# Storing the first tile of a contrast kernel in eight strided pieces with growing packets

## Chip, cores, metric

The kernel runs on one core of a Trainium2 chip. The metric is the device time in microseconds, as a median of runs. The profiled span, from the first instruction to the last, is about 2 us shorter (237.3 us in the run of the kernel before that took 239.14). In the trace, q1 is the queue of loads (issued by SP, the SyncE engine) and q10 the queue of stores (issued by ACT). Both run on the same 16 DMA engines: in the kernel before, their packets sum to 98.9% of 16 engines' span, and about 16 are in flight from 3 to 234 us. A packet is one record of a DMA engine's work in the trace; here it moves one contiguous piece of one row (for tile 0's 128 rows, stored in two column parts, 128 packets of 8 KB and 128 of 24 KB). Packet records lie in the trace file, and no view of the profile prints them one by one; numbers said to be from them were read there.

## The reference

```python
# x: 16 x 3 x 512 x 512 float32, factor = 1.5
mean = np.mean(x, axis=(2, 3), keepdims=True)
return np.clip(mean + factor * (x - mean), 0, 1).astype(np.float32)
```

There are 48 images of 1 MiB. All bytes must come in once and go out once, 100.66 MB in total. An image can be clipped only when all of it has been summed.

## The kernel before

Four images make a tile of 128 rows of 8192 floats (4.19 MB, 32 KB a row), so there are 12 tiles. They pass through a ring of six tile buffers. DVE (VectorE) sums a part of each row, ACT (ScalarE) the rest, PE (TensorE) turns the row sums into one shift per row, and DVE multiplies, adds and clips in place. Tile 0 is clipped and stored in two column parts, 2048 and 6144 wide.

```python
SHORT = 2048
FIRST = (SHORT, ROW - SHORT)
SUM = 4352
# ... (cut)
    def compute(t):
        xt = ring[:, t % BUFS, :]
        own = sums[:, 2 * t : 2 * t + 2]
        nc.vector.tensor_reduce(out=own[:, 0:1], in_=xt[:, 0:SUM], axis=mybir.AxisListType.X, op=Alu.add)
        nc.scalar.activation(out=junk, in_=xt[:, SUM:ROW], func=Act.Copy, accum_out=own[:, 1:2])
        # ... two matmuls into shift (cut)
        c = 0
        for n in FIRST if t == 0 else [ROW]:
            # ... mult-add, then clip, of columns c to c + n (cut)
            store(t, c, c + n)          # nc.scalar.dma_start: ACT issues it
            c += n
# ... (cut)
        load(0, c1=SHORT)               # nc.sync.dma_start: SP issues it
        load(0, c0=SHORT)
        load(1)
        load(2, n=2)                    # two tiles in one DMA
        load(4, n=2)
        for t in range(n_tiles):
            compute(t)
            if t + BUFS < n_tiles:
                load(t + BUFS)          # waits until tile t has left the buffer
```

Of the kernel before, what the change touches and what calls it, by code (L numbers as in the profile page):

```python
# [1 line left out]

# [4 lines left out]


P = 128  # L10
ROW = 8192
BUFS = 6
SHORT = 2048
FIRST = (SHORT, ROW - SHORT)
SUM = 4352


@with_exitstack
def kernel(
    ctx: ExitStack,  # L20
    tc: tile.TileContext,
    x: bass.AP,
    factor: float,
    out: bass.AP,
):



    nc = tc.nc
    f32 = mybir.dt.float32  # L30
    Alu = mybir.AluOpType
    Act = mybir.ActivationFunctionType

    B, C, H, W = x.shape
    n_img, n_pix = B * C, H * W
    ppi = n_pix // ROW
    per_tile = P // ppi
    n_tiles = n_img // per_tile
    assert ppi * ROW == n_pix and per_tile * n_tiles == n_img

    factor = float(factor)
    wconst = (1.0 - factor) / float(n_pix)

    x_f = x.rearrange("b c h w -> (b c h w)")
    out_f = out.rearrange("b c h w -> (b c h w)")

    def dram(ap, t, c0=0, c1=ROW):
        return bass.AP(tensor=ap.tensor, offset=t * P * ROW + c0, ap=[[ROW, P], [1, c1 - c0]])

    consts = ctx.enter_context(tc.tile_pool(name="consts", bufs=1))  # L50
    xpool = ctx.enter_context(tc.tile_pool(name="xpool", bufs=1))
    small = ctx.enter_context(tc.tile_pool(name="small", bufs=1))
    psum = ctx.enter_context(tc.tile_pool(name="psum", bufs=1, space=bass.MemoryType.PSUM))


    sums = small.tile([P, 2 * n_tiles], f32, name="sums")
    junk = small.tile([P, ROW - SUM], f32, name="junk")
    bias = psum.tile([P, n_tiles], f32, name="bias")

    blockw = consts.tile([P, P], f32, name="blockw")  # L60
    nc.gpsimd.memset(blockw, 0.0)  # L61
    for a in range(0, P, ppi):
        nc.gpsimd.memset(blockw[a : a + ppi, a : a + ppi], wconst)  # L63


    ring = xpool.tile([P, BUFS, ROW], f32, name="ring")

    def load(t, c0=0, c1=ROW, n=1):

        b = t % BUFS  # L70
        src = bass.AP(
            tensor=x_f.tensor,
            offset=t * P * ROW + c0,
            ap=[[ROW, P], [P * ROW, n], [1, c1 - c0]],
        )
        nc.sync.dma_start(out=ring[:, b : b + n, c0:c1], in_=src)  # L76
# [4 lines that stand above are left out]
        nc.vector.tensor_reduce(  # L81
            out=own[:, 0:1], in_=xt[:, 0:SUM], axis=mybir.AxisListType.X, op=Alu.add
        )
        nc.scalar.activation(out=junk, in_=xt[:, SUM:ROW], func=Act.Copy, accum_out=own[:, 1:2])  # L84
        shift = bias[:, t : t + 1]
        nc.tensor.matmul(shift, blockw, own[:, 1:2], start=True, stop=False)  # L86
        nc.tensor.matmul(shift, blockw, own[:, 0:1], start=False, stop=True)  # L87
        c = 0
        for n in FIRST if t == 0 else [ROW]:
            part = xt[:, c : c + n]  # L90
            nc.vector.tensor_scalar(  # L91
                out=part, in0=part, scalar1=factor, scalar2=shift, op0=Alu.mult, op1=Alu.add
            )
            nc.vector.tensor_scalar(  # L94
                out=part, in0=part, scalar1=0.0, scalar2=1.0, op0=Alu.max, op1=Alu.min
            )
            store(t, c, c + n)
            c += n

    def store(t, c0, c1):  # L100
        nc.scalar.dma_start(out=dram(out_f, t, c0, c1), in_=ring[:, t % BUFS, c0:c1])

    with tc.manual_schedule():
        load(0, c1=SHORT)
        load(0, c0=SHORT)
        load(1)
        load(2, n=2)
        load(4, n=2)
        for t in range(n_tiles):
            compute(t)  # L110
            if t + BUFS < n_tiles:
                load(t + BUFS)


# [1 line left out]
_INS = ['x', 'factor']  # L116
_OUTS = [((16, 3, 512, 512), 'float32')]

_NUMBERS = {'factor': 1.5}


# [26 lines left out]
```

## Time and profile before

| | kernel before |
|---|---|
| time, median of 3 runs | 239.27 us (239.07 to 239.33) |
| profiled span | 237.3 us |
| DVE busy, idle waiting for loads | 163.1 us, 45.7 us |
| first store issued | 20.91 us |
| ACT starts its sum of tile 1 | 28.08 us |
| last load landed, last clip done | 203.73 us, 218.1 us |

DVE waits for loads in its sums (busy time, mean ns of one | idle time before them):

```profile
L81 DVE TENSOR_REDUCE sums<-ring 128x1 f32<-128x4352 f32 x12 | 56.2, 4683 | 45.7 <-DMA ring<-in_x_dram 45.7
```

These lines of the timeline (start, duration, engine, line, work) are where the change acts:

```profile
20.91 7.06 ACTq L101 DMA_DIRECT2D out_dram<-ring  x2
...
28.08 3.40 ACT L84 ACTIVATE junk<-ring 128x3840 f32<-128x3840 f32 x1 [11.70 <-DVE ring L94]
...
41.94 0.34 ACTq L101 DMA_DIRECT2D out_dram<-ring  x1
```

ACT issues the two stores of tile 0 between 20.91 and 27.97 us, sums its part of tile 1 at once, and issues the store of tile 1 at 41.94 us.

### The profile page before, as it was taken

What the parts mean: (1) busy time and instruction counts of PE and PEld (TensorE: products, weight loads), DVE (VectorE), ACT (ScalarE), POOL (GpSimd) and SP (SyncE); (2) the same over time, 40 slices, a digit from 0 to 9 for tenths busy, and PEclk for the clock granted to TensorE, in tenths of its full rate; (3) what the DMA queues carried; (4) which work ended last, traced back from release to release, by engine and by line L of the source; (5) the groups of instructions that cost most, each with busy time, mean ns of one, the idle gap of its engine ahead of it and who ended that gap; (6) DMA issues with size and microseconds to landing.
All of it is one profiled execution on the core that took longest, in us unless ns stands there. A gap on an engine that the chain in (4) does not pass through costs nothing.

```text
span 237.3 us, 285 instructions
## 1 busy us (share of the span) xinstructions
PE 14.1 (6%) x48; PEld 12.0 (5%) x48; DVE 163.1 (69%) x38; ACT 43.2 (18%) x25; POOL 0.9 (0%) x9
## 2 busy tenths in 40 slices
PE   0010010001010001010010100100100100010000
PEld 0010010001010001010010100100100100010000
DVE  0079989048989328999989898891892795687000
ACT  2050230041050023050320504101400500500000
POOL 1000000000000000000000000000000000000000
DMA  7999999999999999999999999999999999999996
GB/s 297 410 442 442 421 442 359 456 439 441 442 436 414 403 431 442 442 442 442 436 442 436 414 409 425 442 442 442 442 436 442 436 420 403 425 442 442 442 442 265
DMA packets 3712, 100.66 MB, mean 424 GB/s; under 512 B 384, under 2 KB 384, under 8 KB 384
## 3 DMA queue, kind: packets, MB, share of 16 engines
q1 hardware_dynamic: 1840, 50.33, 49.7%
q10 hardware_dynamic: 1872, 50.33, 49.2%
HBM read 50.33 MB, written 50.33 MB: 424 GB/s over the span
## 4 chain that ended last, share of the span: by engine, by line
DMA 57%; DVE 29%; another core or an unknown queue 3%; PE 1%; SPq 1%; issue 0%; DVEq 0%
DMA ring<-in_x_dram 41%; DMA out_dram<-ring 16%; DVE sums L81 10%; DVE ring L91 9%; DVE ring L94 9%; PE bias L87 1%; SPq L76 1%; DVEq L91 0%
## 5 line engine op out<-in xcount | busy, mean ns | idle before, releaser
L81 DVE TENSOR_REDUCE sums<-ring 128x1 f32<-128x4352 f32 x12 | 56.2, 4683 | 45.7 <-DMA ring<-in_x_dram 45.7
L84 ACT ACTIVATE junk<-ring 128x3840 f32<-128x3840 f32 x12 | 40.8, 3403 | 163.3 <-DMA ring<-in_x_dram 107.5
L91 DVE TENSOR_SCALAR ring<-ring,bias 128x8192 f32<-128x8192 f32 (+2 forms) x13 | 54.1, 4163 | 8.9 <-PE bias L87 7.4
L94 DVE TENSOR_SCALAR ring<-ring 128x8192 f32<-128x8192 f32 (+2 forms) x13 | 53.3, 4099 | 0.4
L86 PE MATMUL bias<-sums,blockw 128*128 128x1 f32 x24 | 7.0, 361 | 190.8 <-ACT junk L84 190.8
L86 PEld LDWEIGHTS bias<-sums,blockw 128*128 128x128 f32 x24 | 6.0, 312 | 191.7 <-ACT junk L84 175.2
L87 PE MATMUL bias<-sums,blockw 128*128 128x1 f32 x24 | 7.0, 363 | 4.3 <-DVE sums L81 3.9
L87 PEld LDWEIGHTS bias<-sums,blockw 128*128 128x128 f32 x24 | 6.0, 311 | 5.3 <-DVE sums L81 5.0
L84 ACT ACTIVATION_READ_ACCUMULATOR junk<-ring 128x1 f32 x12 | 2.2, 186 | 0.0
L84 ACT ACT_TABLE_LOAD x1 | 1.3, 1283 | 0.7 <-PEq L129 0.7
L63 POOL MEMSET blockw<- 32x32 f32 x4 | 0.5, 117 | 0.2
L61 POOL MEMSET blockw<- 128x128 f32 x1 | 0.2, 204 | 0.3 <-POOLq L129 0.3
L129 POOL MEMSET const-bfloat16-1.0<- 128x1 bf16 x1 | 0.1, 111 | 0.0
L129 POOL MEMSET const-uint8-127<- 128x1 uint8 x1 | 0.1, 111 | 0.0
L129 POOL MEMSET const-float32-1.0<- 128x1 f32 x1 | 0.1, 108 | 0.0
L129 POOL MEMSET const-float32-0.0<- 128x1 f32 x1 | 0.1, 103 | 0.2 <-issue 0.2
## 6 DMA issues: line engine op xcount, KB each, us to landing
out_dram<-ring ACTq DMA_DIRECT2D x11, 4096.0 KB, 35.8
ring<-in_x_dram SPq DMA_DIRECT2D x7, 4096.0 KB, 49.7
ring<-in_x_dram SPq DMA_DIRECT2D x2, 8192.0 KB, 66.7
ring<-in_x_dram SPq DMA_DIRECT2D x1, 3072.0 KB, 11.7
out_dram<-ring ACTq DMA_DIRECT2D x1, 3072.0 KB, 28.2
ring<-in_x_dram SPq DMA_DIRECT2D x1, 1024.0 KB, 4.8
out_dram<-ring ACTq DMA_DIRECT2D x1, 1024.0 KB, 17.5
```

The lines of the kernel that those rows point to most:

```text
L61: nc.gpsimd.memset(blockw, 0.0)
L63: nc.gpsimd.memset(blockw[a : a + ppi, a : a + ppi], wconst)
L76: nc.sync.dma_start(out=ring[:, b : b + n, c0:c1], in_=src)
L81: nc.vector.tensor_reduce(out=own[:, 0:1], in_=xt[:, 0:SUM], axis=mybir.AxisListType.X, op=Alu.add)
L84: nc.scalar.activation(out=junk, in_=xt[:, SUM:ROW], func=Act.Copy, accum_out=own[:, 1:2])
L86: nc.tensor.matmul(shift, blockw, own[:, 1:2], start=True, stop=False)
L87: nc.tensor.matmul(shift, blockw, own[:, 0:1], start=False, stop=True)
L91: nc.vector.tensor_scalar(out=part, in0=part, scalar1=factor, scalar2=shift, op0=Alu.mult, op1=Alu.add)
L94: nc.vector.tensor_scalar(out=part, in0=part, scalar1=0.0, scalar2=1.0, op0=Alu.max, op1=Alu.min)
L129: nc = _bacc.Bacc("TRN2", target_bir_lowering=False, num_devices=1)
```

## The change

Its intent, as far as the code tells: the first stores meet loads that have the engines to themselves, and small packets should let them in gently. Tile 0 leaves in eight DMAs of 32 rows each (every 4th row), whose packets grow from 4 KB to 32 KB. All are issued after the whole clip. The two paired loads become four single ones.

```diff
-FIRST = (SHORT, ROW - SHORT)
+RAMP = [            # first row, row step, first column, last column
+    (0, 4, 0, 1024),
+    (1, 4, 0, 2048),
+    (0, 4, 1024, 4096),
+    (2, 4, 0, 4096),
+    (2, 4, 4096, ROW),
+    (0, 4, 4096, ROW),
+    (1, 4, 2048, ROW),
+    (3, 4, 0, ROW),
+]
 ... (cut: tile 0's mult-add and clip are no longer split)
+        for piece in RAMP if t == 0 else [(0, 1, 0, ROW)]:
+            store(t, *piece)
-    def store(t, c0, c1):
-        nc.scalar.dma_start(out=dram(out_f, t, c0, c1), in_=ring[:, t % BUFS, c0:c1])
+    def store(t, q=0, parts=1, c0=0, c1=ROW):
+        dst = bass.AP(tensor=out_f.tensor, offset=(t * P + q) * ROW + c0,
+                      ap=[[parts * ROW, P // parts], [1, c1 - c0]])
+        nc.scalar.dma_start(out=dst, in_=ring[q::parts, t % BUFS, c0:c1])
 ... (cut)
-        load(2, n=2)
-        load(4, n=2)
+        for t in range(2, BUFS):
+            load(t)
```

More of the change, by code (lines that the diff above doesn't have):

```diff
@@ L45 @@
     out_f = out.rearrange("b c h w -> (b c h w)")
-    def dram(ap, t, c0=0, c1=ROW):
-        return bass.AP(tensor=ap.tensor, offset=t * P * ROW + c0, ap=[[ROW, P], [1, c1 - c0]])
     consts = ctx.enter_context(tc.tile_pool(name="consts", bufs=1))
@@ L87, in compute @@
         nc.tensor.matmul(shift, blockw, own[:, 0:1], start=False, stop=True)
-        c = 0
-        for n in FIRST if t == 0 else [ROW]:
-            part = xt[:, c : c + n]
-            nc.vector.tensor_scalar(
-                out=part, in0=part, scalar1=factor, scalar2=shift, op0=Alu.mult, op1=Alu.add
-            )
-            nc.vector.tensor_scalar(
-                out=part, in0=part, scalar1=0.0, scalar2=1.0, op0=Alu.max, op1=Alu.min
-            )
-            store(t, c, c + n)
-            c += n
-    def store(t, c0, c1):
-        nc.scalar.dma_start(out=dram(out_f, t, c0, c1), in_=ring[:, t % BUFS, c0:c1])
+        nc.vector.tensor_scalar(
+            out=xt, in0=xt, scalar1=factor, scalar2=shift, op0=Alu.mult, op1=Alu.add
+        )
+        nc.vector.tensor_scalar(
+            out=xt, in0=xt, scalar1=0.0, scalar2=1.0, op0=Alu.max, op1=Alu.min
+        )
+        for piece in RAMP if t == 0 else [(0, 1, 0, ROW)]:
+            store(t, *piece)
+    def store(t, q=0, parts=1, c0=0, c1=ROW):
+        dst = bass.AP(
+            tensor=out_f.tensor,
+            offset=(t * P + q) * ROW + c0,
+            ap=[[parts * ROW, P // parts], [1, c1 - c0]],
+        )
+        nc.scalar.dma_start(out=dst, in_=ring[q::parts, t % BUFS, c0:c1])
     with tc.manual_schedule():
```

## The prediction

> **What bounds the kernel now.** I read the page first for busy shares, then the DMA view, then stretches of time, then the chain, and last the timeline of the first 75 us, where the change is.
>
> From the page, busy time of the engines and the DMA rows:
>
> ```profile
> PE 14.1 (6%) x48; PEld 12.0 (5%) x48; DVE 163.1 (69%) x38; ACT 43.2 (18%) x25; POOL 0.9 (0%) x9
> ...
> DMA  7999999999999999999999999999999999999996
> ...
> DMA packets 3712, 100.66 MB, mean 424 GB/s; under 512 B 384, under 2 KB 384, under 8 KB 384
> ...
> q1 hardware_dynamic: 1840, 50.33, 49.7%
> q10 hardware_dynamic: 1872, 50.33, 49.2%
> ```
>
> No compute engine is above 69%. The loads (q1) take 49.7% and the stores (q10) 49.2% of 16 DMA engines' span: 98.9% of 237.3 us, or 234.7 us. Only the first and the last slice are below 9. The trace's packet records say the same: the first load packet starts at 1.74 us, the last store packet ends at 236.05 us, and in each microsecond from 3 to 234 about 16 packets are in flight. So the transfers never pause.
>
> Is a packet's cost fixed? Three stretches (last columns: share of the 16 engines, GB/s):
>
> ```profile
> 56.00:60.00 4.00, 0.00 (x1) 0.00 (x0) 3.89 (x1) 0.00 (x0) 0.00 (x0) 1.00 0.91 393
> 80.00:84.00 4.00, 0.00 (x0) 0.00 (x0) 0.00 (x0) 0.00 (x0) 0.00 (x0) 1.00 0.91 393
> 172.00:176.00 4.00, 0.00 (x0) 0.00 (x0) 3.97 (x2) 0.00 (x0) 0.00 (x0) 1.00 0.91 393
> ```
>
> A packet is booked where it starts, so 0.91 is no idling: 393 GB/s over 4 us is 48 packets of 32 KB, and 0.91 x 64 engine-us / 48 is 1.21 us each, with DVE busy or idle. The packet records give median 309 ns for 8 KB, 912 ns for 24 KB and 1213 ns for 32 KB, loads and stores alike. A line through them is 7.7 ns + 36.8 ns per KB of 1,000 bytes.
>
> The chain of waits ends in the last tile:
>
> ```profile
> 154.17 49.57 DMA ring<-in_x_dram
> 203.73 0.02 issue
> 203.76 4.70 DVE sums L81
> ...
> 209.18 4.50 DVE ring L91
> 213.69 0.02 issue
> 213.71 4.43 DVE ring L94
> ```
>
> The last load lands at 203.73 us and the last clip ends at 218.1 us. That chain stops at the last compute instruction, but the transfers run on to 236 us. At 218.1 us the engines still owe 18 us x 0.43 MB/us (16 packets of 32,768 bytes in 1.213 us), about 7.7 MB: the last tile (4.19 MB) and most of the one before. So the last compute ends far earlier than it need, and the time is first packet plus packet time plus tail.
>
> [...] the 8 KB store packets of 24.6 to 36.9 us come about 1.52 us apart on an engine, which is 309 + 1213 ns, one store packet per load packet. Small store packets thus yield bandwidth to loads; they do not waste it. [...]
>
> **The change, part by part.**
>
> *Clip of tile 0.* Two mult-adds and two clips (1.29, 1.23, 3.42 and 3.36 us in the timeline) become one of each (4.49 and 4.43 us, from tile 1's rows). The sum falls from about 9.2 to 8.9 us, and tile 0 is clipped at 18.33 + 8.95 = 27.3 us, not 27.5. But the first store leaves at 27.3 instead of 20.91 us. Loads fill those 6.4 us, since one queue alone keeps the engines busy (12 to 21 us had loads only).
>
> *Packets of tile 0's stores.* Before: 128 of 8 KB and 128 of 24 KB, 256 packets. After: eight DMAs of 32 rows, again 256 packets with the same 4.19 MB. By the line above their engine time is identical: (256 x 7.7 ns + 4.19 MB x 36.8 ns per KB) / 16 is 9.8 us in both. The two 8 MB loads become four of 4 MB; their packets stay 32 KB. Added are 32 DMAs' completion writes instead of 24, one of 9 ns per engine each: 8 x 9 ns = 0.07 us.
>
> *Waits at issue.* In the built program the DMAs share eight completion semaphores in turn, and a DMA waits for the earlier user of its own. With six more stores these waits move into ACT's queue: the sixth piece waits for the load of tile 1, the seventh for the first piece to land, the eighth for the third. ACT works in order, so tile 1's reduction stands behind the eighth piece. I replayed one DMA engine by hand, alternating load and store packets with the durations above, and with 3.7 us from issue to a store's first packet (before: issue 20.91, first packet 24.64). It lands piece one at about 34, piece three at 40.5 and piece eight at 61 us. So ACT starts tile 1 near 41 us instead of 28.08, and tile 1's store is issued near 41 + 4.9 (ACT start to mult-add, 28.08 to 32.95) + 9 = 55 us instead of 41.94. That is 13 us lost on compute. But piece eight's packets last to about 60 us, and on the load side tiles 3, 4 and 5 (issued after the first load, tile 2 and piece two land, about 6, 32 and 37 us) last to 70 us. Neither queue dries.
>
> *Loads 6 on.* Load 6 waits for all of tile 0 to have left, about 61 us instead of 56. Load 5 then still has some 9 us of packets. In return tile 4 need no longer wait for a paired load: before, an 8.20 us wait ended at 87.56 us. Tile 4 should be loaded by about 60 us and DVE should lead again by tile 5.
>
> *Sum.* Nothing is saved in packet time, +0.07 us of completion writes, first packet and tail as they are: 239.27 + 0.1 = about 239.4 us.
>
> **The rivals.** (a) *The smaller first packets help*: loads get ahead, compute starts earlier, and time falls. For it: the DVE idles 45.7 us on loads. Against it: what is idle is not the bound; the most that a perfect order could win is 237.3 - 234.5 (all packets on 16 engines) = 2.8 us, 1.2%, and 1.74 us of it is before the first packet, which the change doesn't touch. It would make 238.5 us. (b) *ACT's new wait becomes the bound*: 13 us lost on tile 1 reach the end if both queues run dry. Against it: the queued loads last past 70 us, and the end has slack: tile 11 could be clipped 9 us later and still be stored in time. With this wholly on the path the time would be 250 us; I give it 2%. (c) *The 32-row stores run slower*: no trace here says which rows go to which engine. [...] Worst case every packet of tile 0's stores takes twice as long: +9.8 us. [...] I give any visible loss 12%. (d) *Unequal engines*: if the rows spread unevenly, some engines end late; two rows on each make this unlikely.
>
> **Range and chances.** Three runs of before lie within 0.26 us, and the packet sum admits no gain beyond 1.2%, so faster by over 2% is nearly excluded: 0.01. Slower by over 2% (over 244 us) needs (b) or a bad (c): 0.03. The rest, 0.96, is the same. The range reaches down 0.6 us for another order at the tail or another chip, and up 1 us for a mild (c): 238.8 to 240.4 us.
>
> **What would show it right or wrong.** Right: q1 plus q10 near 234.6 us of 16 engines; every DMA slice between the first and the last at 9; the first store issued near 27.4 us; ACT's second reduction starting near 41 us and tile 1's mult-add with it, later than 32.95; tile 2's reduction following late, but tile 4's no longer waiting until 87 us; the last load landing within 4 us of 203.7. Wrong: a slice below 9 between 30 and 75 us (b), or store packets of 16 KB taking visibly more than 0.61 us and q10's share above 49.5% (c). A span shorter by over 1 us would mean that packet time isn't fixed, contrary to my central step.

The sum came to 239.27 + 0.1 = about 239.4 us. The records have these numbers. Between 25.3 and 36.6 us of the kernel before, 118 load packets of 32 KB (3.87 MB) and 126 store packets of 8 KB (1.03 MB) start, together 0.43 MB/us. The records of issue name eight semaphores (100 to 102 and 106 to 110) for its 24 DMAs, and the same eight for the 32 of the changed kernel. Completion writes are records of 4 bytes and 9 ns, 16 for each DMA (384 before, 512 after). That a piece of 32 rows puts two packets on each engine was seen in the changed kernel alone (below).

## The result, and the profile after

The changed kernel takes 239.30 us (median of 6 runs, 239.06 to 239.50) against 239.23 us of the kernel before in the same rounds. All runs were fast, that is, none was over 1.5% above the fastest of its kernel. The ratio is 1.0003, with a 95% interval of 0.999 to 1.0016. (Ratios are the mean time of one kernel's fast runs over that of the other's in the same rounds, so not quite the ratio of the medians quoted.) The time is the same.

The DMA rows of the changed kernel's page answer to those of the prediction:

```profile
DMA  7999999999999999999999999999999999999996
...
DMA packets 3841, 100.67 MB, mean 424 GB/s; under 512 B 512, under 2 KB 512, under 8 KB 544
...
q1 hardware_dynamic: 1872, 50.33, 49.7%
q10 hardware_dynamic: 1968, 50.33, 49.2%
```

The shares of loads and stores are those of before, and again every slice but the first and last is full. (Of the 129 packets more, 128 are completion writes (8 DMAs more, 16 records of 4 B each), and one is a record of another queue, q14; the data packets are as many as before.)

The inside is not the same at all. The timeline, ACT only:

```profile
27.25 17.32 ACTq L112 DMA_DIRECT2D out_dram<-ring  x8
44.62 3.40 ACT L92 ACTIVATE junk<-ring 128x3840 f32<-128x3840 f32 x1 [28.37 <-DMA out_dram<-ring]
...
58.27 0.36 ACTq L112 DMA_DIRECT2D out_dram<-ring  x1
```

Issuing eight stores holds ACT for 17.32 us, because the last ones wait for a semaphore that an earlier piece frees: the seventh (semaphore 107, like the first) is issued at 35.93 us, when the first has landed (35.91), the eighth (109, like the third) at 44.09, when the third has (44.07). Tile 1's sum starts 16.5 us later than before, and tile 1's store is issued 16.3 us later. Yet the end of the chain of waits has moved the other way:

```profile
166.28 26.43 DMA ring<-in_x_dram
192.71 0.02 issue
192.73 4.70 DVE sums L89
...
202.69 4.43 DVE ring L99
```

The last load lands at 192.71 us, not 203.73, and the last clip ends at 207.1 us, not 218.1. The groups' idle times agree:

```profile
L96 DVE TENSOR_SCALAR ring<-ring,bias 128x8192 f32<-128x8192 f32 x12 | 53.9, 4491 | 25.7 <-PE bias L95 22.7
L89 DVE TENSOR_REDUCE sums<-ring 128x1 f32<-128x4352 f32 x12 | 56.2, 4681 | 18.6 <-DMA ring<-in_x_dram 18.6
```

DVE's idle time on loads (the last number of the second line, L89; it was L81 before) has shrunk from 45.7 to 18.6 us. A new wait on PE (and so on ACT's late sum) of 17.5 us at tile 1 stands beside it. All compute is done 11 us sooner, and the time hasn't moved.

**Why the loads finish sooner.** Stores begin later: their first packet starts at 31.38 us instead of 24.64. Then tile 0 takes longer to leave, from 31.4 to 69.2 us (it was 24.6 to 55.9). The packet records show why. They don't number the engines, but the 3,328 data packets line up in 16 chains, each packet within a few ns of the end of the one before (median 4), with two packets of each piece of 4, 8, 12 and 24 KB in every chain; and each of the 19 stores has 16 completion records. So each piece puts two packets on each engine. Twelve engines send theirs at about the same time; the other four come up to 2.6 us later. The next piece starts on no engine before these four have started their last packet: 34.36 us after 34.15, 38.60 after 38.54, 43.74 after 43.10, and so on at every seam. Between the first packets of piece one (about 31.5 us) and of piece eight (about 61.4) a leading engine sends 14 store packets, 7.3 us by their durations. The other 22.5 us are 18.6 load packets' worth, where one load packet per store packet would give 14. (Before, with 16 engines in near step and two DMAs of eight packets each on an engine, it was one per store packet: 8 KB store packets came 1.52 us apart, 309 + 1213 ns.) What holds the twelve back at a seam the records don't say. While tile 0 leaves slowly, loads get the rest. By the packet records the changed kernel has loaded 23.9 MB by 69.2 us, and the kernel before 21.5 MB. The engines move 0.43 MB/us, and beside stores the loads get half of it (30.9 of 60.8 MB from 60 to 200 us in the kernel before); at that rate the lead of 2.5 MB is worth 11.4 us, an estimate from these numbers. The measured lead is 11 us.

Later runs (below) show which of the two counts. In the changed kernel the last packet of tile 0 ends at 67.6 us and the last load packet at 191.15; in the kernel before at 54.3 and 202.16. With tile 0 in two DMAs, issued as late as the eight, they end at 59.1 and 197.03, and with tile 0 whole, in one DMA as late, at 53.0 and 207.48. So a later first store does not by itself bring the loads forward; what goes with it is how long tile 0 takes to leave. (The single loads in place of paired ones are in all of these but the kernel before. No run takes that part alone.)

### The profile page after: what moved, and what is told of

It reads as the page before. It is cut to its first block, busy times and chain, and to the rows that moved or that the text cites. A ratio compares the mean times of both kernels' runs of the same rounds, so it can differ in the third digit from the quotient of the medians.

```text
span 237.3 us, 298 instructions
## 1 busy us (share of the span) xinstructions
PE 13.9 (6%) x48; PEld 12.0 (5%) x48; DVE 162.4 (68%) x36; ACT 43.2 (18%) x25; POOL 0.9 (0%) x9
## 4 chain that ended last, share of the span: by engine, by line
DMA 54%; DVE 19%; another core or an unknown queue 8%; issue 3%; PE 2%; SPq 1%; ACT 0%; ACTq 0%; DVEq 0%
DMA ring<-in_x_dram 35%; DMA out_dram<-ring 19%; DVE ring L96 8%; DVE ring L99 7%; DVE sums L89 4%; PE bias L95 1%; SPq L84 1%; PE bias L94 0%; ACT junk L92 0%; ACTq L112 0%; DVEq L96 0%; ACTq L92 0%
## 5 line engine op out<-in xcount | busy, mean ns | idle before, releaser
L96 DVE TENSOR_SCALAR ring<-ring,bias 128x8192 f32<-128x8192 f32 x12 | 53.9, 4491 | 25.7 <-PE bias L95 22.7
L89 DVE TENSOR_REDUCE sums<-ring 128x1 f32<-128x4352 f32 x12 | 56.2, 4681 | 18.6 <-DMA ring<-in_x_dram 18.6
L99 DVE TENSOR_SCALAR ring<-ring 128x8192 f32<-128x8192 f32 x12 | 53.1, 4428 | 0.4
```

Source lines behind the costliest of these rows:

```text
L96: nc.vector.tensor_scalar(out=xt, in0=xt, scalar1=factor, scalar2=shift, op0=Alu.mult, op1=Alu.add)
L99: nc.vector.tensor_scalar(out=xt, in0=xt, scalar1=0.0, scalar2=1.0, op0=Alu.max, op1=Alu.min)
```

## The experiments

Theory: 16 DMA engines are busy from the first packet to the last, the time is the sum of packet times, and what moves inside is slack. Rivals: the wait on ACT has a price that something else pays back; the row pattern matters; the size of the first packets matters.

### The slack: more work on the last tile, both kernels

```diff
-            (the clip, once)
+            for _ in range(5 if t == n_tiles - 1 else 1):
+                (the clip)
```

The edit is the same in both kernels, and a clip repeated gives the same result.

> The kernel before, with the clip of the last tile done five times instead of once (same result): 4 x 4.43 = 17.7 us more VectorE work after the last load. Theory (transfers bind, and compute has slack only until the store queue runs dry): the last clip ends at 218.1 + 17.7 = 235.8 us, past the end of all other transfers at about 226.5, so the last tile's store of 9.7 us starts alone at about 237.5: span near 248, time near 250 us. Rival (compute is hidden anyway): 239.3 us.

> The changed kernel with the same four more clips on the last tile. Its last clip ended at 207.1 us, 11.0 us earlier than in the kernel before. Theory (the change bought 11 us of slack that the time doesn't show): last clip at 224.8 us, while the store queue lasts until about 226.3, so 239.3 to 240.5 us, some 10 us less than the kernel before with the same load. Rival (the two kernels are alike wherever it counts): it loses as much as the kernel before does, about 250 us.

The kernel before then takes 250.37 us (ratio 1.0464), the changed one 239.78 us (ratio 1.0021, interval 1.0006 to 1.0036). The span and DMA row of each page, first the kernel before with the longer tail:

```profile
span 248.0 us, 289 instructions
...
DMA  7999999999999999999999999999999999993087
```

and the changed kernel with it:

```profile
span 237.5 us, 302 instructions
...
DMA  7999999999999999999999999999999999999996
```

In the first, the digits 3 and 0 are DMA engines with nothing to do, waiting for the last tile's store, which is issued after the clip, at 236.08 us. In the second, the last store is issued at 225.36 us, while earlier stores still fill the engines. So the earlier loads are worth 10.6 us (250.37 to 239.78), but only to a kernel whose last tile needs longer. This one did not, and so saw nothing of it.

### ACT's wait taken away

Three pieces are issued after tile 1's sum on ACT instead of before.

```diff
-        for piece in RAMP if t == 0 else [(0, 1, 0, ROW)]:
+        for piece in RAMP[:5] if t == 0 else [(0, 1, 0, ROW)]:
             store(t, *piece)
 ... and in compute(1), after the ACT sum:
+        if t == 1:
+            for piece in RAMP[5:]:
+                store(0, *piece)
+            load(BUFS)                 # in its place after the stores of tile 0
```

> The changed kernel with its last three pieces issued after tile 1's reduction on ACT, so that the semaphore waits of these pieces no longer hold tile 1 back. Theory (the wait is real but hidden: 16.5 us on ACT, none in the time): ACT's second reduction starts near 28 to 31 us instead of 44.62, tile 1's store is issued near 42 to 46 us instead of 58.27, and the time stays 239.3 us within 0.3. Rival (the wait costs something that the small packets win back): the time falls by 1 us or more, below 238.3.

Measured: 239.11 us, ratio 1.0002 (0.9985 to 1.0018). The timeline of ACT shows the wait gone from tile 1 and moved behind its sum:

```profile
27.23 3.16 ACTq L116 DMA_DIRECT2D out_dram<-ring  x5
30.49 3.40 ACT L92 ACTIVATE junk<-ring 128x3840 f32<-128x3840 f32 x1 [14.27 <-issue]
32.36 0.48 ACTq L116 DMA_DIRECT2D out_dram<-ring  x1
...
35.85 13.57 ACTq L116 DMA_DIRECT2D out_dram<-ring  x3
```

Tile 1's sum starts at 30.49 us, 14.1 us sooner, and neither the time nor the last load packet (191.17 us, against 191.15) moves. One part of the expectation missed: tile 1's store could not go at 42 to 46 us. It is the third issue of the last line (after pieces seven and eight) and went at 49.06 us, since, by the times, it shares its semaphore with the fourth piece, which landed at 48.98. The wait is free here, and it isn't what brought the loads forward either.

### Three buffers instead of six

The same wait where the load queue is too short to hide it: a ring of 3 tiles, for the kernel before, the changed one, and the changed one with the three pieces after tile 1's sum.

```diff
-BUFS = 6
+BUFS = 3        # and only the first three tiles are loaded ahead
```

> The kernel before with a ring of 3 tiles instead of 6. With 3 buffers the load queue runs dry once three tiles are in, near 33 us, so waits on stores and compute reach the transfers: DMA slices below 9, some 250 us (240 to 260).

> The changed kernel with a ring of 3 tiles. Theory (the later first store and ACT's wait are hidden only by queued loads): now they show, and it is slower than the kernel before with the same ring by 3 to 10 us. Rival (the wait on ACT never reaches the transfers): the two differ by less than 1 us.

> The changed kernel with a ring of 3 and the last three pieces issued after tile 1's reduction on ACT. If ACT's wait is what the short ring exposes, this wins back more than half of what the changed kernel loses with a ring of 3; if the later first store is, it wins back nearly nothing.

Their medians are 248.80, 254.20 and 251.81 us. By the ratios of the fast runs to the kernel before with six buffers (1.039, 1.0598, 1.0534), the changed kernel now loses 2.0% to the kernel before at the same ring, about 5 us (1.0598 / 1.039; one of its four runs, of 256.58 us, is slow and left out). Moving the three pieces makes 0.6% of difference, which is not clear of the noise: the intervals, 1.0533 to 1.0664 and 1.0513 to 1.0554, overlap. The DMA rows, in the same order:

```profile
DMA  7999998999999989999999999999999999999295
```

```profile
DMA  7999987999999999999999999999999999999277
```

```profile
DMA  7999987999999999999999999999999999989177
```

Two gaps show: near 30 to 45 us (digits 8 and 7), where the loads have run out and the stores come late, and at the end. By the packet records the engines idle 0.9, 2.1 and 2.2 us between 30 and 46 us, and 5.6, 6.7 and 6.7 us after 190 us. So what the six buffers hide is real. That it is ACT's wait is not shown: the edit brings tile 1's sum from 37.33 to 33.93 us (27.98 in the kernel before), and neither gap closes. Little of it is the leaving of tile 0, whose buffer is loaded anew at 42.63, 43.38 and 43.50 us. Most of the delay appears at tile 1's buffer, loaded anew at 61.07, 66.35 and 66.42 us. What causes it these runs do not divide.

### Which rows a piece takes

```diff
-            offset=(t * P + q) * ROW + c0, ap=[[parts * ROW, P // parts], [1, c1 - c0]],
+            offset=(t * P + q * (P // parts)) * ROW + c0, ap=[[ROW, P // parts], [1, c1 - c0]],
-        in_=ring[q::parts, t % BUFS, c0:c1]
+        in_=ring[q * (P // parts) : (q + 1) * (P // parts), t % BUFS, c0:c1]
```

> The changed kernel with the eight pieces of tile 0 taken from 32 adjacent rows each (rows 0-31, 32-63 and so on) instead of every 4th row. Theory (a packet costs 7.7 ns + 36.8 ns per 1,000 bytes whatever rows it reads): 16 KB pieces stay at 611 ns, stores stay at 49.2% of the engines' span, time 239.3 us within 0.3. Rival [...]: the pieces' packets take up to twice as long (16 KB about 1.2 us), up to 9.8 us of engine time more, stores above 50%, time 241 to 249 us.

Measured: 241.22 us, ratio 1.0078 (1.0052 to 1.0103). Adjacent rows do cost about 1.9 us. But the packets do not double: 4, 8 and 16 KB pieces keep 159, 309 and 611 ns, and only the 24 KB piece stretches, from 912 ns to 1106 in the mean. Some load packets beside the stores stretch as well, now and then up to 170 us. Half of the loss is such longer packets (by the packet records 0.9 us per engine more than in the changed kernel). The rest is that the engines end unevenly, which shows in stretches at the end (last columns: share of the engines, GB/s), first of the changed kernel:

```profile
234.00:236.00 2.00, 0.00 (x0) 0.00 (x0) 0.00 (x0) 0.00 (x0) 0.00 (x0) 1.00 0.61 262
236.00:238.00 2.00, 0.00 (x0) 0.00 (x0) 0.00 (x0) 0.00 (x0) 0.00 (x0) 1.00 0.00 0
```

and of the one with adjacent rows:

```profile
234.00:236.00 2.00, 0.00 (x0) 0.00 (x0) 0.00 (x0) 0.00 (x0) 0.00 (x0) 1.00 0.95 410
236.00:238.00 2.00, 0.00 (x0) 0.00 (x0) 0.00 (x0) 0.00 (x0) 0.00 (x0) 1.00 0.16 66
```

Packets still start after 236 us, on a few engines, while the rest are done. For these eight pieces every 4th row is therefore worth its index arithmetic (1.9 us). Why adjacent rows cost more, no run shows.

### How large the first store packets are

Four variants of the list of tile 0's pieces, all issued after the whole clip:

```diff
-        for piece in RAMP if t == 0 else [(0, 1, 0, ROW)]:
+        for piece in [(0, 1, 0, ROW)]:                                    # whole
+        RAMP = [(0, 4, 0, ROW), (1, 4, 0, ROW), (2, 4, 0, ROW), (3, 4, 0, ROW)]   # quarters
+        RAMP = [(0, 1, 0, 2048), (0, 1, 2048, ROW)]                       # two
+        for piece in RAMP[::-1] if t == 0 else [(0, 1, 0, ROW)]:          # reversed
```

> The changed kernel with tile 0 stored whole, in one DMA of 128 packets of 32 KB after its clip, no pieces. Theory (only packet time counts; 128 packets fewer x 7.7 ns / 16 is 0.06 us): 239.2 us within 0.3, every DMA slice full, tile 1's reduction on ACT near 28 us, but the last load landing well after 192.7 us, since stores take half of the engines from 31 us on: about 203 to 210 us. Rival (how tile 0 leaves decides the time): more than 1 us above 239.3.

> The changed kernel with tile 0 in four DMAs of every 4th row, each with whole rows (32 packets of 32 KB), so no growing packets. Storing tile 0 whole cost 1.1 us: load packets of 28 to 31 us took up to 3.2 us instead of 1.21. Theory A (large first store packets are what disturbs): this one loses as much, about 240.3 us. Theory B (128 rows at once disturb, 32 at a time do not): 239.3 us within 0.3, and no load packet above 2 us.

> The changed kernel with tile 0 in two DMAs of all 128 rows, 8 KB and then 24 KB packets, both after the whole clip (the packets of the kernel before, the issue time and the loads of the changed one). Theory A (small first packets are what counts): 239.3 us within 0.3. Theory B (32 rows at a time are): about 240.3 us. Either way the issue time of 27.3 instead of 20.9 us costs nothing.

> The changed kernel with its eight pieces issued in the opposite order: 32 KB packets first, 4 KB last. Same pieces, same bytes, same packets. Theory A (the size of the first store packets, met by loads that run alone, is what disturbs): load packets of 28 to 32 us take 1.5 to 3 us as in the runs with tile 0 stored whole and in quarters, and the time rises by 1 to 5 us, to 240.3 to 244. Theory B (the order of the packets doesn't matter, the sum of packet times does): 239.3 us within 0.3.

| tile 0 leaves as | first packets | median us | ratio (95% interval) | longest load packet, 27 to 33 us |
|---|---|---|---|---|
| eight, growing (the change) | 4 KB | 239.30 | 1.0003 (0.999 to 1.0016) | 1.50 us |
| eight, shrinking | 32 KB | 239.79 | 1.0029 (1.0014 to 1.0044) | 2.86 us |
| whole | 32 KB | 240.50 | 1.0046 (1.0029 to 1.0063) | 3.18 us |
| four quarters by rows | 32 KB | 243.90 | 1.0202 (1.0182 to 1.0221) | 2.54 us |
| two, by columns | 8 KB | 239.4 in fast runs | 1.0009 (0.9994 to 1.0023) | 1.63 us |

Whole, my expectation of 239.2 us missed: it costs 1.1 us. (That the last load would land late, at 203 to 210 us, held: 209.15.) The stretch from 28 to 32 us shows where, first in the changed kernel, then with tile 0 whole, in quarters and reversed:

```profile
28.00:32.00 4.00, 0.00 (x0) 0.00 (x0) 3.82 (x1) 0.00 (x0) 0.00 (x0) 1.00 1.01 434
```

```profile
28.00:32.00 4.00, 0.54 (x2) 0.50 (x2) 4.00 (x1) 3.41 (x2) 0.00 (x0) 1.00 1.08 319
```

```profile
28.00:32.00 4.00, 0.00 (x0) 0.00 (x0) 4.00 (x1) 2.03 (x1) 0.00 (x0) 1.00 0.94 287
```

```profile
28.00:32.00 4.00, 0.00 (x0) 0.00 (x0) 3.86 (x1) 0.00 (x0) 0.00 (x0) 1.00 0.99 287
```

The engines are as busy (share near 1), but move 287 to 319 GB/s instead of 434. Load packets of 27 to 33 us, when 32 KB stores set in, took up to 2.54, 2.86 and 3.18 us instead of 1.21. So packet time was not quite a constant: it stretched where the stores began, and more with 32 KB packets first than with 4 or 8 KB (1.50 and 1.63 us). It stretched again later, which the table's window leaves out: to 1.79 us at 38 us in the kernel before, as the 24 KB packets set in, and to 1.89 us at 42 us in the changed one, at the seam before the 16 KB pieces. The reversed list is the clean test, since it has the same pieces in another order. It loses 0.3%, clear of zero but below the 1 us that I had put as the least. Small first packets mattered, then, for about 0.7 us; eight pieces are not needed for it, as two with 8 KB in front do as well in fast runs.

The quarters lose 4.7 us, more than either theory allowed. Their engines drift apart: load packets of 1.3 to 2.4 us recur until 173 us, most of them near 75, 133 and 171 us, and the last sixteen packets end between 237.5 and 240.7 us, when those of the changed kernel end between 235.6 and 236.0. Why rows by quarters without growing packets set this off, and the other two large starts much less, stays open.

Of the variant with two pieces three of six runs took 247.84 to 254.67 us and are slow; its plain median of 243.67 us mixes both. No profile of a slow run exists and the granted clock was 1.0 in all, so I don't explain them. The kernel before, on the same chip, had none in 11 runs, and the changed kernel none in its 6. Six runs are too few to say that the eight pieces protect from it.

### Packets of 4 KB everywhere

```diff
-    ring = xpool.tile([P, BUFS, ROW], f32, name="ring")
+    ring = xpool.tile([P, BUFS, ROW // BLK, BLK + GAP], f32, name="ring")    # BLK = 1024, GAP = 8
 ... and all accesses of the ring by blocks of BLK; SUM = 5120
```

> The changed kernel with 8 floats of padding after every 1024 in the ring, so that every load and store of every tile moves in 4 KB packets: the same bytes in 24,576 packets (VectorE sums 5120 and ACT 3072 of a row, for space). The 4 KB packet took 159 ns. Theory (the time is the sum of packet times over 16 engines): 24,576 x 159 ns / 16 = 244.2 us of packets instead of 234.5, so +9.7, about 249 us. Rival (packet overhead hides, only bytes count): 239.3 us.

Measured: 245.07 us, ratio 1.0243 (1.0229 to 1.0258). The DMA row and the queues of its page (packets, MB, share of 16 engines):

```profile
DMA  6999999999999999999999999999999999999997
...
q1 hardware_dynamic: 12496, 50.33, 50.6%
q10 hardware_dynamic: 12592, 50.33, 50.3%
```

The engines are full here too, so it is not the other split of the sums that binds. More packets of the same bytes did cost time, and the rival falls. But they cost 5.9 us, not 9.7. The shares sum to 100.9% of the engines: records of neighbouring packets overlap, and 159 ns are not all its own. The kernel before and the changed one have 3,328 data packets, this one 24,576. That is 1,328 more per engine, so a packet more costs 5.9 us / 1,328 = 4.4 ns, not the 7.7 ns of my line.

## Why the prediction was right, and where it was not

**The bound: right.** Time, shares of both queues and full slices are as foretold, and the two experiments with a longer tail show from both sides that compute is slack until the store queue runs dry. The remark that tile 11 could be clipped 9 us later holds in kind: 17.7 us more cost the kernel before 11.1 us, so its slack was about 6.6.

**Packets of tile 0's stores: right for this change, for 256 packets replace 256.** The term of 7.7 ns per packet was mis-sized; 4.4 ns was measured. And a fixed cost of a packet left out that packets stretched where the stores began. Both kernels start with small packets, and by the records both lose about 0.8 us per engine to packets above their usual length after the first 6 us, so this cancels. I had not foreseen either half of it: that the sum came out is luck here. Had the change been from two pieces to one, I would have missed 1.1 us.

**Clip and first issue: right.** The first store left at 27.25 us (foretold 27.3). The prediction's sum for the clip before is slightly off: 1.29 + 1.23 + 3.42 + 3.36 is 9.3 us, not 9.2, and the last of them ended at 27.61 us, not 27.5.

**Waits at issue: right in kind, mis-sized.** The pieces landed at 35.91 (first), 44.07 (third) and 69.19 us (eighth), where I had 34, 40.5 and 61. So ACT lost 16.5 us, not 13, and tile 1's store went at 58.27, not 55. The replay alternated load and store without a break, and with all engines in step. It missed that four engines lag and that the others wait for them at each seam: 24 of the first piece's 32 packets start by 31.9 us, the last four at 34.0 to 34.2, and the piece lands at 35.91.

**Queues don't run dry: right.** Load 6 was issued at 69.34 us (foretold 61) and load 5 landed at 76.56 us. With six buffers taking the wait away changes nothing; with three the change costs 2.0%, of which ACT's wait is not shown to be a part.

**Loads 6 on: wrong in one number.** "The last load landing within 4 us of 203.7" failed; it landed at 192.71. I had followed load 6's delay, but not that the slow leaving of tile 0 hands its share to the loads. Tile 4 did land when foretold (58.70 us, "by about 60"), and its sum waits for no load; it still starts at 86.75 us (87.58 before), since DVE is busy with tile 3 until then.

**Rivals.** (a) happened to compute and gave nothing to the time, as argued; its 238.5 us does not follow from its numbers, since 2.8 - 1.74 us would make 238.2, and 1.2 us of the 2.8 come after the last packet. (b) does not show with six buffers, and with three it is not separated from the rest. (c) is not in this kernel, as its pieces keep their packet times, but it is half right for adjacent rows (1.9 us; 24 KB packets took 1106 ns instead of 912, the smaller ones their usual time).

## What to carry to other kernels

Where, as here, the DMA engines are busy from first to last, a wait that is added or taken away is not worth its length in the time, only in slack (here ACT's sum of tile 1 came 16.5 us later, the last clip 11 us sooner, and the time moved by 0.07 us): find how long the transfers still run after the last compute, and add work there to see whether slack was won. When stores set in beside loads, try small packets first (0.7 us here; 8 KB did in fast runs, but three of those six runs were slow), and when a tile is cut by rows, try rows a few apart (1.9 us here, with pieces that grow; without growing they cost 4.7 us). A store on an engine that also computes can hold its next work back through a semaphore it shares (16.5 us here), which six buffers hid.
